# Two-layer hybrid decoder trunk: the first layer reads x channels first, scales by the norm's factors at the evictions, and runs its first chunk by rows of weights

## The chip, the cores and the metric

The kernel runs on one core of a Trainium2 chip. The metric is the device time of one execution in microseconds (us). Before the change three runs took 711.84, 712.14 and 716.08 us (median 712.14 us). TensorE is PE in the profile, VectorE is DVE, ScalarE is ACT, GpSimd is POOL, and SP is the engine whose queue issues the DMAs. TensorE's clock is granted at one of two levels, 1.2 or 2.4 GHz; the profile writes them as 0.5 and 1.0.

## The reference

The input x has 512 tokens of 1024 channels. Two layers follow each other, and each begins with an RMS norm and one wide projection:

```python
def rmsnorm(x, g, eps=RMS_EPS):
    xf = x.astype(jnp.float32)
    y = xf * lax.rsqrt(jnp.mean(xf * xf, axis=-1, keepdims=True) + eps)
    return (y * g.astype(jnp.float32)).astype(x.dtype)
...
    u = rmsnorm(h, norm_gain) @ w_in
    qa, ka, va, ga, qd, kd, vd, gd = jnp.split(u, list(np.cumsum(IN_SPLITS)[:-1]), axis=-1)
```

The eight parts have 512 columns each. Queries and keys get a partial rotation (rope) and feed two kinds of attention (a dilated window, "a", and a differential one, "d"); the values va and vd are multiplied by the attention weights; ga and gd gate the results through silu. An output projection, a second norm with a gate projection, and a small embedding product end the layer. A last norm ends the kernel. The norm multiplies each token by one factor (the inverse root mean square of its channels) and each channel by one gain, so that rmsnorm(h) @ w_in is the same as (h * gain) @ w_in with every token's row of the result multiplied by that token's factor.

## The kernel before

**Tiles.** The contraction over 1024 channels is cut into 8 blocks of 128 (kb). A weight *row* r is 256 input channels by 512 columns (kb 2r and 2r+1), 512 KB in one DMA; a *chunk* is four such rows. Each float32 number is split into a high part in TensorE's float32r form and a low part, the rest. A product takes three matmuls (high by high, high by low, low by high). A *unit* is one 128 x 512 result, 8 blocks of 3 matmuls, 24 in all. It is accumulated in one PSUM bank; units alternate between banks 0 and 1, and all else takes the other six banks in turn through `bank()`.

**Where a row goes.** SP loads it to a staging buffer (`stg`; the fourth load of all goes to `of`). ACT copies it to float32r (high part, 128 x 1024 at once), and then DVE or POOL subtracts (low part, in two halves of 128 x 512) into one of five slots of `ring`. A staging buffer is loaded again once both halves of its low part are done. `emit_loads` and `chunk` set this up. In the very first chunk DVE takes one half of each row and POOL the other; in later chunks POOL takes seven halves of eight.

**The order of chunks** is `SEQ`: vd (values), d0 and d1 (queries and keys of the differential heads), va, a0, a1, then the gates, the output projection (o0, o1) and the second norm's projection (p0, p1); 48 units in each layer, plus the attention of the heads in between.

**The order of instructions.** All operations are recorded first, with planned times (`pe` and `at`), and then `Machine.schedule` puts them in order with a list of costs of its own and replays them. So every instruction stands at line 286 of the profile (L286), and tiles name them. Within an engine instructions run in that fixed order; one that waits holds up those behind it.

**The start.** `warm_up` runs matmuls on zeros. SP loads x token by token (`load_x`, 128 tokens x 1024 channels each, tile `fr`), the norm's gain as one row, and the weights. `sumsq` and `rstd` make the token's factor: sums of squares on ACT and DVE, then a power of -0.5 on POOL (`st<-st 128x1`). `first_gain` spreads the gain over the partitions with POOL's partition_broadcast. `xn` multiplies x by factor and gain on DVE, TensorE transposes the result in 8 groups of 4 (`b<-idt,fr`), and ACT and DVE write its high and low parts to the tile `xy` (`norm_T`). Only then can the first chunk's matmuls run, a unit for each group of 128 tokens, and token group 1's norm is worked while unit 0 runs, and so on. The units of d0 come out with channels on the partitions; `qk_done` multiplies them by cos and sin tables, `v_done` splits the values, `gate_done` forms silu.

**Queues.** SP issues all DMAs in order. It holds at most eight open: each waits for the one eight places before it.

Of the kernel before, what the change touches and what calls it, by code (L numbers as in the profile page):

```python
# [312 lines left out]


def trunk(tc, x, p, attn_gain, w_in, w_out, lq1, lk1, lq2, lk2, subln, ple_gain, w_gate, w_ple,
          final_gain, tables, out):
    nc = tc.nc
    x2 = x.rearrange("b s d -> (b s) d")
    out2 = out.rearrange("b s d -> (b s) d")
# [4 lines left out]
    with tc.tile_pool(name="sb", bufs=1) as sb, tc.tile_pool(name="ps", bufs=1, space=PSUM) as psp, \  # L324
# [10 lines left out]
        OF = sb.tile([128, 8, 512], F32, name="of")  # L335
        MISC = sb.tile([128, 3, 512], F32, name="misc")
        CT = sb.tile([128, 4, 512], F32, name="ct")
        IDT = sb.tile([128, 128], F32, name="idt")
        ST = sb.tile([128, 192], F32, name="st")
        hsave = drp.tile([S, D], F32, name="hsave")  # L340
# [5 lines left out]
        GSUB = [ST[:, 8 + l:9 + l] for l in range(DEPTH)]  # L346
        SS = ST[:, 16:32]
        RS = ST[:, 32:36]
        VAR = ST[:, 36:40]
        DST = ST[:, 40:56]  # L350
        HST = ST[:, 64:128]
        GROW = MISC[0:1, 1:3, :].rearrange("p a n -> p (a n)")
        FRB = FR.rearrange("p (b n) -> p b n", n=512)

        def H(t, h):
# [53 lines left out]
        def emit_loads():  # L409
            order = sorted(range(len(loads)), key=lambda i: loads[i][:2])  # L410
            for n, i in enumerate(order):
                t, us, src, hi, lo, eng = loads[i]
                st = stage(n)

                def load(st=st, src=src):
                    SPQ.dma_start(st, src)

                def high(st=st, hi=hi):
                    ACT.activation(hi, st, AF.Copy)

                def low(k, st=st, hi=hi, lo=lo, eng=eng):
                    eng[k].tensor_sub(lo[:, k], st[:, k], hi[:, k])
                if n <= NSTG:
                    at(-10, 55.0 + 0.1 * n, load)
# [9 lines left out]
        def chunk(s0, src, k0=0):  # L434
            slots = {}
            for r in range(4):
                slot = npair[0] % NPAIR
                npair[0] += 1
                row = (r + k0 // 2) % 4
                slots[row] = slot  # L440
                if s0 == 0:
                    t, us = -10, 64.7 + 1.4 * r
# [38 lines left out]
        def rstd(t):  # L481
            DVE.tensor_scalar(VAR[:, t:t + 1], SS[:, 2 * t:2 * t + 1], SS[:, 2 * t + 1:2 * t + 2],
                              EPS, op0=OP.add, op1=OP.add)
            POOL.tensor_tensor(RS[:, t:t + 1], VAR[:, t:t + 1], NHALF[:, 0:1], op=OP.pow)

        def xn(t, h, gain):
            DVE.scalar_tensor_tensor(XN(t, h), H(t, h), RS[:, t:t + 1],
# [28 lines left out]
        def setup():  # L516
            DVE.memset(PT[:, 0, 0:512].bitcast(F32), 0.0)
            DVE.memset(NHALF, -0.5)
            for i in range(2):
                for e in range(2):  # L520
                    POOL.memset(QK[64 - 64 * e:128 - 64 * e, i, 4 + e].bitcast(F32), 0.0)
            ACT.activation(ST[:, 132:136], NHALF, AF.Exp)
            make_identity(nc, IDT)

        def load_x(t, h=None):
            cols = slice(0, D) if h is None else slice(512 * h, 512 * h + 512)
            SPQ.dma_start(HT(t)[:, cols], x2[t * 128:(t + 1) * 128, cols])

        def load_first_gain():
            SPQ.dma_start(GROW, attn_gain[0].unsqueeze(0))  # L530

        def first_gain():
            POOL.partition_broadcast(GN[0], GROW)


        def warm_up():
# [31 lines left out]
            at(-10, 60 + us, f, *a)  # L568

        st(-9, setup)  # L570
        st(-8, load_x, 0, 0)
        st(-7, load_x, 0, 1)
        st(-6, load_first_gain)
        for t in range(1, T):
            st((-4.75, -4, -3)[t - 1], load_x, t)
# [4 lines left out]
        st(2.0, first_gain)  # L580
        pe(-3, 6.0, warm_up)
        pe(-0.05, 1.2, lambda: None)
        for h in range(2):
            st(2.0 + 0.6 * h, sumsq, 0, h, (ACT, DVE)[h])
        norm_T(-10, 63.2, -0.9, 0, GN[0], 0)
        for t in range(1, T):
            for h in range(2):
                at(t - 1, 0.1 * h, sumsq, t, h, (ACT, DVE)[h])
            norm_T(t - 1, 1.0, t - 0.2, t, GN[0], 0)


        nP = [0]
# [174 lines left out]
        SHUF = list(range(8, 16)) + list(range(8)) + list(range(16, 32))  # L767
        nrt = [0]

        def qk_done(pr, isk):  # L770
            def done(t, o):
                r = {}
                buf = QK[:, pr % 2]

                def rot1():
                    r[0] = RT[nrt[0] % 2]
                    nrt[0] += 1
                    DVE.stream_shuffle(r[0][1], o, SHUF)
                    DVE.tensor_mul(r[0][0], o, C)

                def rot2():
                    POOL.tensor_mul(r[0][1], r[0][1], SN)
# [34 lines left out]
        def v_done(view, nh):  # L817
            def done(t, o):
                src = o.rearrange("p (h d) -> p h d", h=nh)

                def hi():
                    ACT.activation(view[:, :, 0, :], src, AF.Copy)

                def lo():
                    DVE.tensor_sub(view[:, :, 1, :], src, view[:, :, 0, :])
                at(t, 0.05, hi)
                at(t, 0.6, lo)
            return done

        def gate_done(kb, ureg, lo_from):  # L830
            def done(t, o):
                sg = MISC[:, 2, :]

                def f():
                    ACT.activation(sg, o, AF.Tanh, scale=0.5)
                    DVE.scalar_tensor_tensor(sg, sg, 1.0, o, op0=OP.add, op1=OP.mult)

                def g():
                    DVE.tensor_mul(OF[:, kb, :], OF[:, kb, :], sg)
# [75 lines left out]
        for l in range(DEPTH):  # L915
# [5 lines left out]
            def qk_chunk(name, g):  # L921
                s0 = at_of[name]
                w = chunk(s0, wi[CHUNK[name]])
                for n, c in enumerate((0, 2, 1, 3)):
                    unit(s0 + n, w, X, "col", c, qk_done(2 * g + n // 2, n % 2))

            def v_chunk(name, view, nh):
                s0 = at_of[name]
                w = chunk(s0, wi[CHUNK[name]])
                for t in range(T):  # L930
                    unit(s0 + t, w, X, "tok", t, v_done(view(Y, t), nh))

            def g_chunk(name, kb0):
                s0 = at_of[name]
                w = chunk(s0, wi[CHUNK[name]])
                for i in range(4):
                    unit(s0 + i, w, X, "col", i, gate_done(kb0 + i, Y, B + QA[7] + LP + 0.2))

            def o_chunk(name, h):
                s0 = at_of[name]  # L940
# [134 lines left out]
```

## Time and profile before

| | |
|---|---|
| median of three runs | 712.14 us (711.84 to 716.08) |
| the profiled execution | 715.25 us |
| its span, first to last instruction | 713.1 us |
| PE busy | 680.4 us, 95% of the span, 3379 matmuls and transposes |
| DVE, ACT, POOL busy | 428.0, 370.3, 359.7 us |
| mean granted clock of TensorE | 0.977 |

The span and 2.1 us around it make the profiled execution's own time. TensorE is busy in nearly all of the span. Busy time is an average over the whole program; the change's instructions stand in the first 80 us, apart from the evictions of layer 0.

### The profile page before, as it was taken

Reading aid. Unit: us, or ns where it says so; the run is one execution under the profiler, and the core shown is the slowest. Engines: PE = TensorE matmul, PEld = TensorE weight load, DVE = VectorE, ACT = ScalarE, POOL = GpSimd, SP = SyncE. Lnnn points to the kernel's source line nnn. Section 1 sums busy time; section 2 is a strip of 40 time slices with the busy share of each in tenths; the row PEclk is TensorE's granted clock in tenths of the full one; section 3 lists DMA queues with packets and bytes.
Section 4 is the critical chain, followed back from the end, with each engine's and each line's share of the span. In section 5 each row is a group of like instructions: output and inputs, shape, how many; then the busy total and the mean of one; then the engine's idle time right before and its main releaser. Section 6 shows DMA issues by size and latency. Waiting matters only on the chain.

```text
span 713.1 us, 9718 instructions
## 1 busy us (share of the span) xinstructions
PE 680.4 (95%) x3379; PEld 573.3 (80%) x3379; DVE 428.0 (60%) x855; ACT 370.3 (52%) x803; POOL 359.7 (50%) x279
## 2 busy tenths in 40 slices
PE   2399999999999999999999999999999999999995
PEld 1288888888888888888888888888888888888885
DVE  1573599675776573373364279976587657248244
ACT  2243556664887852443353255674578885244321
POOL 2327858086661343861552776717746154376122
PEclk7599999999999999999999999999999999999998
DMA  8214455134443354430432445414454344353002
GB/s 300 68 60 132 124 149 158 30 119 119 125 125 105 125 179 139 149 116 33 148 111 95 148 140 127 130 48 145 121 129 128 101 142 153 119 176 95 24 30 89
DMA packets 30883, 84.79 MB, mean 119 GB/s; under 512 B 5617, under 2 KB 5617, under 8 KB 30834
## 3 DMA queue, kind: packets, MB, share of 16 engines
q1 hardware_dynamic: 30834, 84.17, 38.5%
q8 instruction: 26, 0.43, 0.2%
q14 instruction: 23, 0.19, 0.1%
HBM read 63.18 MB, written 4.19 MB: 94 GB/s over the span
## 4 chain that ended last, share of the span: by engine, by line
PE 93%; issue 3%; DVE 2%; DMA 1%; POOL 0%; SPq 0%; POOLq 0%; ACT 0%; DVEq 0%
PE b L286 93%; DVE fr L286 2%; DMA stg<-in_w_in_dram 1%; SPq L286 0%; POOL of L286 0%; DVE pt L286 0%; DVE misc L286 0%; POOL st L286 0%; DVE of L286 0%; DVE ring L286 0%; POOLq L1071 0%; DVE st L286 0%; ACT of L286 0%; DVEq L1071 0%; POOLq L286 0%
## 5 line engine op out<-in xcount | busy, mean ns | idle before, releaser
L286 POOL TENSOR_TENSOR ring<-stg,ring 128x512 fp32r<-128x512 f32 x164 | 233.9, 1452 | 205.9 <-ACT ring L286 205.5
L286 PE MATMUL b<-xy,ring 128*128 128x512 f32 x1152 | 285.7, 394 | 0.0
L286 PE MATMUL b<-ring,xy 128*128 128x512 f32 (+1 forms) x1176 | 279.7, 391 | 0.0
L286 PEld LDWEIGHTS b<-ring,xy 128*128 128x128 f32 x1176 | 215.8, 189 | 41.6 <-DVE fr L286 0.2
L286 PEld LDWEIGHTS b<-xy,ring 128*128 128x128 f32 x1152 | 211.0, 188 | 39.1
L286 ACT ACTIVATE ring<-stg 128x1024 fp32r<-128x1024 f32 x95 | 100.0, 1058 | 55.0 <-PE b L286 39.4
L286 ACT ACTIVATE fr<-fr,st 128x128 f32<-128x128 f32 (+3 forms) x193 | 102.0, 556 | 34.3 <-DVE st L286 31.6
L286 DVE CUSTOM_DVE_ANT_0 fr<-b,ct 128x512 f32<-128x512 f32 (+3 forms) x128 | 58.4, 484 | 36.3 <-PE b L286 35.6
L286 PE MATMUL b<-idt,fr 128*128 128x128 f32 x368 | 53.2, 277 | 23.4 <-DVE fr L286 23.3
L286 POOL TENSOR_TENSOR fr<-fr,ct 128x512 f32<-128x512 f32 x32 | 44.4, 1386 | 57.0 <-DVE fr L286 57.0
L286 PEld LDWEIGHTS b<-idt,fr 128*128 128x128 f32 x368 | 45.2, 143 | 33.9 <-DVE fr L286 24.6
L286 DVE SCALAR_TENSOR_TENSOR fr<-fr,st,of 128x512 f32<-128x512 f32 (+1 forms) x39 | 44.0, 1161 | 25.8 <-POOL st L286 25.8
L286 ACT ACTIVATE xy<-b 128x512 fp32r<-128x512 f32 x48 | 28.3, 593 | 52.9 <-PE b L286 52.5
L286 DVE TENSOR_TENSOR ring<-stg,ring 128x512 fp32r<-128x512 f32 x26 | 32.6, 1253 | 36.5 <-ACT ring L286 36.5
L286 POOL TENSOR_TENSOR st<-st 128x1 f32<-128x1 f32 (+1 forms) x29 | 20.8, 718 | 63.3 <-DVE st L286 47.8
L286 PE MATMUL b<-qk 128*128 128x128 f32 (+3 forms) x256 | 52.7, 324 | 0.0
L286 DVE TENSOR_TENSOR pt<-b,pt 128x384 fp32r<-128x384 f32 (+1 forms) x72 | 40.0, 593 | 11.7 <-ACT pt L286 11.3
L286 POOL TENSOR_TENSOR fr<-fr 128x512 f32<-128x512 f32 x32 | 45.1, 1415 | 2.6 <-DVE fr L286 1.0
L286 ACT ACTIVATE fr<-fr 128x512 f32<-128x512 f32 x35 | 22.0, 629 | 46.6 <-DVE fr L286 44.3
L286 DVE TENSOR_TENSOR xy<-b,xy 128x512 fp32r<-128x512 f32 x48 | 32.4, 683 | 19.5 <-ACT xy L286 19.5
L286 ACT ACTIVATE pt<-b 128x384 fp32r<-128x384 f32 (+1 forms) x72 | 34.4, 524 | 18.2 <-PE b L286 18.1
L286 PEld LDWEIGHTS b<-qk 128*128 128x128 f32 x256 | 39.3, 190 | 4.0 <-issue 0.2
(62 smaller groups left out, 547.4 us busy)
## 6 DMA issues: line engine op xcount, KB each, us to landing
stg<-in_w_in_dram SPq DMA_DIRECT2D x63, 512.0 KB, 3.4
qk<-nt SPq DMA_DIRECT2D x128, 128.0 KB, 2.3
stg<-in_w_out_dram SPq DMA_DIRECT2D x16, 512.0 KB, 4.6
stg<-in_w_ple_gate_dram SPq DMA_DIRECT2D x16, 512.0 KB, 3.4
fr<-in_x_dram SPq DMA_DIRECT2D x7, 512.0 KB, 5.4
stg<-in_w_ple_dram SPq DMA_DIRECT2D x4, 512.0 KB, 3.3
hsave<-fr SPq DMA_DIRECT2D x4, 512.0 KB, 2.6
fr<-hsave SPq DMA_DIRECT2D x4, 512.0 KB, 3.4
```

The costliest lines, as they stand in the source:

```text
L286: getattr(self.eng[e], op)(*args, **kw)
```

## The change

The first layer no longer normalises x before its projection. The host hands x over a second time, transposed (`xt`, 128 x 8 x 512, channels on the partitions), and the gain with channels on the partitions (`gt`, 128 x 8, 32 bytes a partition). ACT writes the high part of x times gain straight into `xy`, DVE the low part. x by tokens is still loaded, for the sums of squares alone (`x_sumsq`). The factors of the tokens (`RS0`) are applied where the results leave PSUM: in `v_done` as a scale of each partition; for queries, keys and gates, where tokens lie along the free dimension, POOL puts the factors on the diagonals of four 128 x 128 matrices, four matmuls with a matrix of ones spread them over the partitions, and the cos and sin tables (`C0`, `SN0`) and a plain copy (`RB`) take them in (`spread_rstd`). Gates of layer 0 get one more DVE product. partition_broadcast, the eight groups of transposes and their evictions in layer 0 are gone. The first chunk runs by rows of weights: four PSUM banks are open, one for each token group, and each weight row is used for all four before the next. The warm-up has 14 matmuls in place of 11.

```diff
-        NWARM = 11
+        NWARM = 14
...
+        def units_by_rows(w, ureg, dones):
+            o = [BANK[0], BANK[1], bank(), bank()]
+            def part(r, t):
+                for kb in (2 * r, 2 * r + 1):
+                    for n, (ul, wl) in enumerate(PASSES):
+                        mm(o[t], UT(ureg, ul, kb)[:, t * 128:(t + 1) * 128], w(wl, kb),
+                           start=(kb == 0 and n == 0), stop=(kb == KB - 1 and n == 2))
+            for r in range(4):
+                for t in range(T):
+                    pe(r + 0.25 * t, 1.362, part, r, t)
+            for t in range(T):
+                dones[t](3.2 + 0.25 * t, o[t])
...
-        def first_gain():
-            POOL.partition_broadcast(GN[0], GROW)
+        def load_gt():
+            SPQ.dma_start(GT, gt)
+        def load_xt(r):
+            SPQ.dma_start(FRB[:, 2 * r:2 * r + 2, :], xt[:, 2 * r:2 * r + 2, :])
+        def xt_hi(kb):
+            ACT.activation(UT(0, 0, kb), FRB[:, kb, :], AF.Copy, scale=GT[:, kb:kb + 1])
+        def xt_lo(kb):
+            DVE.scalar_tensor_tensor(UT(0, 1, kb), FRB[:, kb, :], GT[:, kb:kb + 1], UT(0, 0, kb),
+                                     op0=OP.mult, op1=OP.subtract)
...
+        def spread_rstd():
+            b = bank()
+            for t in range(T):
+                diag = MISC[:, 1, t * 128:(t + 1) * 128]
+                POOL.tensor_scalar(diag, IDT, RS0[:, t:t + 1], None, op0=OP.mult)
+            for t in range(T):
+                mm(b[:, t * 128:(t + 1) * 128], ONES, MISC[:, 1, t * 128:(t + 1) * 128], start=True, stop=True)
+            ACT.activation(RB, b, AF.Copy)
+            DVE.tensor_mul(C0, C, b)
+            DVE.tensor_mul(SN0, SN, b)
...
-            norm_T(t - 1, 1.0, t - 0.2, t, GN[0], 0)
+                st(3.1 + 0.3 * t, x_sumsq, t, h)
+            st(3.2 + 0.3 * t, rstd, t, RS0)
+        pe(2.5, 1.9, spread_rstd)
...
-                    ACT.activation(view[:, :, 0, :], src, AF.Copy)
+                    ACT.activation(view[:, :, 0, :], src, AF.Copy, **({} if rs is None else {"scale": rs}))
...
+                    if l == 0:
+                        g = RT[1][kb % 2]
+                        DVE.tensor_mul(g, o, RB)
```

**PE, from the first instruction.** `pt` is the warm-up's zeros, `idt,fr` a transpose of x, `ring,xy` a matmul of the first chunk (vd), and the number after `b_` the PSUM bank. Before:

```order
L286 MATMUL b_79<-pt 128x512 x11
L286 MATMUL b_80<-idt,fr 128x128 x4
L286 MATMUL b_81<-idt,fr 128x128 x4
L286 MATMUL b_77<-ring,xy_63 128x512 x9
L286 MATMUL b_82<-idt,fr 128x128 x4
L286 MATMUL b_77<-ring,xy_63 128x512 x12
```

After, at the same place (the four groups of 6 are weight row 0 for the four token groups; rows 1 to 3 repeat them):

```order
L286 MATMUL b_84<-pt 128x512 x14
L286 MATMUL b_80<-ring,xy_63 128x512 x6
L286 MATMUL b_81<-ring,xy_63 128x512 x6
L286 MATMUL b_82<-ring,xy_63 128x512 x6
L286 MATMUL b_83<-ring,xy_63 128x512 x6
```

The transposes are gone, and the first real matmul needs one row of weights and two blocks of xt where it needed a normalised and transposed x.

**POOL, from the same place.** `qk` is a memset, the ISA row ahead of `of<-misc` and the one behind it reload POOL's code library around partition_broadcast, `st<-st` is the power that gives a token group's factors, `ring` a low half of weights. Before:

```order
L286 MEMSET qk 64x512 x3
L286 ISA
L286 ISA of<-misc 128x1024 [waits DMAHW2_49,Pool_49]
L286 ISA
L286 TENSOR_TENSOR st<-st 128x1 [waits DVE_49]
L286 TENSOR_TENSOR ring<-stg,ring 128x512 [waits DMAHW3_49,Activation_49]
```

After, the rows that follow the memset and the halves of the first chunk; the first four `ring` rows are the first two rows of d0, `misc<-idt,st` is a diagonal:

```order
L286 TENSOR_TENSOR ring<-stg,ring 128x512 [waits DMAHW2_49,Activation_49]
L286 TENSOR_TENSOR ring<-stg,ring 128x512
L286 TENSOR_TENSOR ring<-stg,ring 128x512 [waits DMAHW0_49,PE_49,Activation_49]
L286 TENSOR_TENSOR ring<-stg,ring 128x512 [waits PE_49]
L286 TENSOR_TENSOR st<-st 128x1 [waits DVE_49]
L286 TENSOR_SCALAR misc<-idt,st 128x128 [waits Pool_49]
L286 TENSOR_TENSOR st<-st 128x1 [waits DVE_49]
L286 TENSOR_SCALAR misc<-idt,st 128x128 [waits Pool_49]
L286 TENSOR_TENSOR ring<-stg,ring 128x512 [waits DMAHW3_49,PE_49,Activation_49]
L286 TENSOR_TENSOR ring<-stg,ring 128x512 [waits PE_49]
```

Both library reloads are gone, and the factors of token groups 2 and 3 stand between the second and the third weight row of d0.

**ACT, at the end of the first chunk after the change.** `xy_64<-b,st` is the eviction of a token group of vd with its factor, `ring<-stg` the high part of a weight row of d0, `fr,st<-fr` a sum of squares of token groups 2 and 3:

```order
L286 ACTIVATE xy_64<-b_81,st 128x4x128
L286 ACTIVATE ring<-stg 128x1024
L286 ACTIVATE fr,st<-fr 128x512 x2
L286 ACTIVATE xy_64<-b_82,st 128x4x128
L286 ACTIVATE xy_64<-b_83,st 128x4x128
L286 ACTIVATE ring<-stg 128x1024 x2
```

The evictions of groups 2 and 3, which wait for their factors, stand ahead of the third and fourth weight row of d0.

From the gates of layer 0 on, and in all of layer 1, PE's rows stand in the same order as before.

## Rows read from the trace of the kernel before

**Rows 1.** The page: span, and the clock in 40 equal slices (tenths of full speed).

```profile
span 713.1 us, 9718 instructions
...
PEclk7599999999999999999999999999999999999998
```

**Rows 2.** The waits of PE in the whole span: engine, line, waited for, us in total, times, longest.

```profile
PE b L286 <- DVE fr L286: 23.3, 2, 22.8
```

**Rows 3.** The timeline of the first 30 us: start, duration, engine, operation, out<-in, count, and idle time before it with what ended it.

```profile
1.47 4.30 PE L286 MATMUL b<-pt 128*128 128x512 f32 x11 [1.47 <-DVE pt L286]
1.57 2.20 POOL L286 MEMSET qk<- 64x512 f32 x4
...
14.48 1.30 POOL L286 PARTITION_BROADCAST of<-misc  x1 [10.71 <-issue]
...
26.12 0.59 POOL L286 TENSOR_TENSOR st<-st 128x1 f32<-128x1 f32 x1 [10.33 <-issue]
...
26.74 3.43 DVE L286 SCALAR_TENSOR_TENSOR fr<-fr,st,of 128x512 f32<-128x512 f32 x2 [17.69 <-POOL st L286]
...
28.55 1.11 PE L286 MATMUL b<-idt,fr 128*128 128x128 f32 x4 [22.78 <-DVE fr L286]
```

**Rows 4.** The timeline of PE from the first chunk to the second units of d0.

```profile
31.00 4.19 PE L286 MATMUL b<-ring,xy 128*128 128x512 f32 x9
34.98 0.84 PE L286 MATMUL b<-idt,fr 128*128 128x128 f32 x4
...
42.29 0.60 PE L286 MATMUL b<-idt,fr 128*128 128x128 f32 x4
...
42.64 2.33 PE L286 MATMUL b<-ring,xy 128*128 128x512 f32 x9
...
57.12 0.84 PE L286 MATMUL b<-xy,ring 128*128 128x512 f32 x3
...
58.48 16.71 PE L286 MATMUL b<-xy,ring 128*128 128x512 f32 x73
```

**Rows 5.** The same timeline further on, two rows.

```profile
74.80 5.60 PE L286 MATMUL b<-xy,ring 128*128 128x512 f32 x24
80.24 1.43 PE L286 MATMUL b<-qk 128*128 128x128 f32 x8
```

**Rows 6.** Stretches of the start: its length, busy time of PE, PEld, DVE, ACT, POOL (x instructions), granted clock, DMA share, GB/s.

```profile
7.00:8.00 1.00, 0.00 (x0) 0.00 (x0) 0.25 (x1) 0.72 (x1) 0.00 (x0) 1.00 1.06 426
8.00:9.00 1.00, 0.00 (x0) 0.00 (x0) 1.00 (x3) 0.72 (x2) 0.00 (x0) 0.58 0.97 385
...
34.00:35.00 1.00, 1.00 (x4) 0.61 (x4) 1.00 (x2) 0.00 (x0) 0.30 (x1) 0.50 0.00 0
35.00:36.00 1.00, 1.00 (x7) 0.96 (x6) 1.00 (x3) 0.14 (x1) 0.00 (x0) 0.77 0.30 37
36.00:37.00 1.00, 1.00 (x6) 0.82 (x5) 1.00 (x3) 1.00 (x3) 0.00 (x0) 1.00 0.80 287
```

**Rows 7.** The timeline of the first 20 us where it shows a landing: ACT's instructions that waited for a DMA, and SP's issues, each of which went out when the transfer eight places before it had landed.

```profile
4.10 0.63 ACT L286 ACTIVATE fr<-fr 128x512 f32<-128x512 f32 x1 [1.88 <-DMA fr<-in_x_dram]
...
6.66 1.06 ACT L286 ACTIVATE ring<-stg 128x1024 fp32r<-128x1024 f32 x1 [1.84 <-DMA stg<-in_w_in_dram]
...
8.16 0.63 ACT L286 ACTIVATE fr<-fr 128x512 f32<-128x512 f32 x1 [0.45 <-DMA fr<-in_x_dram]
...
9.44 1.06 ACT L286 ACTIVATE ring<-stg 128x1024 fp32r<-128x1024 f32 x1 [0.55 <-DMA stg<-in_w_in_dram]
...
10.72 0.33 SPq L286 DMA_DIRECT2D misc<-in_lambda_q_dram  x1
12.02 0.33 SPq L286 DMA_DIRECT2D misc<-in_lambda_k_dram  x1
13.28 0.33 SPq L286 DMA_DIRECT2D misc<-in_lambda_q_dram  x1
...
14.55 0.33 SPq L286 DMA_DIRECT2D misc<-in_lambda_k_dram  x1
15.98 0.33 SPq L286 DMA_DIRECT2D misc<-in_lambda_q_dram  x1
17.22 0.33 SPq L286 DMA_DIRECT2D misc<-in_lambda_k_dram  x1
17.59 1.83 SPq L286 DMA_DIRECT2D st<-in_subln_gain_dram  x2
```

**Rows 8.** Groups of instructions, shapes kept apart: busy us in all, mean ns of one, idle before them.

```profile
L286 POOL TENSOR_TENSOR ring<-stg,ring 128x512 fp32r<-128x512 f32 x164 | 233.9, 1452 | 205.9 <-ACT ring L286 205.5
L286 ACT ACTIVATE of<-b,st 128x512 f32<-128x512 f32 x8 | 5.5, 686 | 12.0 <-PE b L286 11.9
L286 DVE TENSOR_TENSOR fr<-b,ct 128x512 f32<-128x512 f32 x32 | 21.6, 676 | 0.2
masks.py:199 POOL TENSOR_SCALAR_AFFINE_SELECT idt<-idt 128x128 f32<-128x128 f32 x1 | 0.3, 292 | 0.3 <-POOL idt masks.py:197 0.3
```

**Rows 9.** The timeline: two DVE products with two operands in SBUF, the first beside a POOL product, the second not.

```profile
31.42 1.74 DVE L286 SCALAR_TENSOR_TENSOR fr<-fr,st,of 128x512 f32<-128x512 f32 x1
...
35.97 0.74 DVE L286 SCALAR_TENSOR_TENSOR fr<-fr,st,of 128x512 f32<-128x512 f32 x1
```

More of the change, by code (lines that the diff above doesn't have):

```diff
@@ L315, in trunk @@
 def trunk(tc, x, p, attn_gain, w_in, w_out, lq1, lk1, lq2, lk2, subln, ple_gain, w_gate, w_ple,
-          final_gain, tables, out):
+          final_gain, tables, xt, gt, out):
     nc = tc.nc
@@ L337, in trunk @@
         CT = sb.tile([128, 4, 512], F32, name="ct")
+        CR = sb.tile([128, 3, 512], F32, name="cr")
+        ONES = sb.tile([128, 128], F32, name="ones")
+        GT = sb.tile([128, KB], F32, name="gt")
         IDT = sb.tile([128, 128], F32, name="idt")
@@ L348, in trunk @@
         RS = ST[:, 32:36]
+        RS0 = ST[:, 136:140]
         VAR = ST[:, 36:40]
@@ L351, in trunk @@
         HST = ST[:, 64:128]
-        GROW = MISC[0:1, 1:3, :].rearrange("p a n -> p (a n)")
+        C0, SN0, RB = (CR[:, i, :] for i in range(3))
         FRB = FR.rearrange("p (b n) -> p b n", n=512)
@@ L423, in emit_loads @@
                 if n <= NSTG:
-                    at(-10, 55.0 + 0.1 * n, load)
+                    at(-10, 54.05 + 0.1 * n, load)
                 else:
@@ L479, in sumsq, with rstd @@
                                          op0=OP.mult, op1=OP.add, accum_out=acc)
-        def rstd(t):
+        def rstd(t, to=RS):
             DVE.tensor_scalar(VAR[:, t:t + 1], SS[:, 2 * t:2 * t + 1], SS[:, 2 * t + 1:2 * t + 2],
                               EPS, op0=OP.add, op1=OP.add)
-            POOL.tensor_tensor(RS[:, t:t + 1], VAR[:, t:t + 1], NHALF[:, 0:1], op=OP.pow)
+            POOL.tensor_tensor(to[:, t:t + 1], VAR[:, t:t + 1], NHALF[:, 0:1], op=OP.pow)
         def xn(t, h, gain):
@@ L522, in setup, with load_x, x_sumsq @@
             ACT.activation(ST[:, 132:136], NHALF, AF.Exp)
+            POOL.memset(ONES, 1.0)
             make_identity(nc, IDT)
[L525 to L530, printed above, removed]
-        def first_gain():
-            POOL.partition_broadcast(GN[0], GROW)
+        def load_gt():
[7 more added lines that the diff above has]
+                                     op0=OP.mult, op1=OP.subtract)
+        def load_x(t):
+            SPQ.dma_start(FR[:, 4096 + 1024 * (t % 2):5120 + 1024 * (t % 2)], x2[t * 128:(t + 1) * 128, :])
+        def x_sumsq(t, h):
+            v = FRB[:, 8 + 2 * (t % 2) + h, :]
+            acc = SS[:, 2 * t + h:2 * t + h + 1]
+            if h:
+                ACT.activation(v, v, AF.Square, scale=1.0 / 32, accum_out=acc)
+            else:
+                DVE.tensor_tensor_reduce(v, v, v, scale=1.0 / D, scalar=0.0, op0=OP.mult, op1=OP.add,
+                                         accum_out=acc)
+        def spread_rstd():
[8 more added lines that the diff above has]
+            DVE.tensor_mul(SN0, SN, b)
         def warm_up():
@@ L570, in trunk @@
         st(-9, setup)
[L571 to L575, printed above, removed]
+        st(-8.5, load_gt)
+        for r in range(4):
+            st(-6 + 0.1 * r, load_xt, r)
         at(0, 0.5, load_tables, 0)
@@ L579, in trunk @@
         at(3.5, 0, lambdas)
-        st(2.0, first_gain)
         pe(-3, 6.0, warm_up)
[L582 to L586, printed above, removed]
+        for kb in range(KB):
+            st(2.0 + 0.1 * kb, xt_hi, kb)
+            st(2.05 + 0.1 * kb, xt_lo, kb)
+        for t in range(T):
+            st(3.0 + 0.3 * t, load_x, t)
             for h in range(2):
-                at(t - 1, 0.1 * h, sumsq, t, h, (ACT, DVE)[h])
-            norm_T(t - 1, 1.0, t - 0.2, t, GN[0], 0)
+                st(3.1 + 0.3 * t, x_sumsq, t, h)
+            st(3.2 + 0.3 * t, rstd, t, RS0)
+        pe(2.5, 1.9, spread_rstd)
         nP = [0]
@@ L768, in trunk, with qk_done @@
         nrt = [0]
-        def qk_done(pr, isk):
+        def qk_done(pr, isk, l):
+            cos, sin = (C, SN) if l else (C0, SN0)
             def done(t, o):
@@ L778, in rot1 @@
                     DVE.stream_shuffle(r[0][1], o, SHUF)
-                    DVE.tensor_mul(r[0][0], o, C)
+                    DVE.tensor_mul(r[0][0], o, cos)
                 def rot2():
-                    POOL.tensor_mul(r[0][1], r[0][1], SN)
+                    POOL.tensor_mul(r[0][1], r[0][1], sin)
                     POOL.tensor_add(r[0][0], r[0][0], r[0][1])
@@ L815, in qk_done, with v_done @@
             return done
-        def v_done(view, nh):
+        def v_done(view, nh, rs):
             def done(t, o):
@@ L821, in hi @@
                 def hi():
-                    ACT.activation(view[:, :, 0, :], src, AF.Copy)
+                    ACT.activation(view[:, :, 0, :], src, AF.Copy, **({} if rs is None else {"scale": rs}))
                 def lo():
-                    DVE.tensor_sub(view[:, :, 1, :], src, view[:, :, 0, :])
+                    if rs is None:
+                        DVE.tensor_sub(view[:, :, 1, :], src, view[:, :, 0, :])
+                    else:
+                        DVE.scalar_tensor_tensor(view[:, :, 1, :], src, rs, view[:, :, 0, :],
+                                                 op0=OP.mult, op1=OP.subtract)
                 at(t, 0.05, hi)
@@ L828, in v_done, with gate_done @@
             return done
-        def gate_done(kb, ureg, lo_from):
+        def gate_done(kb, ureg, lo_from, l):
             def done(t, o):
@@ L834, in f @@
                 def f():
-                    ACT.activation(sg, o, AF.Tanh, scale=0.5)
-                    DVE.scalar_tensor_tensor(sg, sg, 1.0, o, op0=OP.add, op1=OP.mult)
+                    g = o
+                    if l == 0:
+                        g = RT[1][kb % 2]
+                        DVE.tensor_mul(g, o, RB)
+                    ACT.activation(sg, g, AF.Tanh, scale=0.5)
+                    DVE.scalar_tensor_tensor(sg, sg, 1.0, g, op0=OP.add, op1=OP.mult)
                 def g():
@@ L929, in v_chunk @@
                 w = chunk(s0, wi[CHUNK[name]])
+                dones = [v_done(view(Y, t), nh, None if l else RS0[:, t:t + 1]) for t in range(T)]
+                if s0 == 0:
+                    units_by_rows(w, X, dones)
+                    return
                 for t in range(T):
-                    unit(s0 + t, w, X, "tok", t, v_done(view(Y, t), nh))
+                    unit(s0 + t, w, X, "tok", t, dones[t])
             def g_chunk(name, kb0):
@@ L1064 @@
     arrays, args = {}, []
-    for name in _INS + ["tables"]:
-        a = const_tables() if name == "tables" else layout(name, inputs[name])
+    for name in _INS + ["tables", "xt", "gt"]:
+        if name == "xt":
+            a = np.ascontiguousarray(np.asarray(inputs["x"])[0].T.reshape(KB, 128, S).transpose(1, 0, 2))
+        elif name == "gt":
+            a = np.ascontiguousarray(np.asarray(inputs["attn_norm_gain"])[0].reshape(KB, 128).T)
+        else:
+            a = const_tables() if name == "tables" else layout(name, inputs[name])
         arrays[f"in_{name}_dram"] = a
```

6 lines of the change are left out of this document (3 added, 3 removed).

## The prediction

> **What bounds the kernel now.** I read the page first: the span is 713.1 us, and the clock row has its low figures in the first slices and the last [rows 1]. Then PE's waits: of 23.3 us in all, one wait of 22.8 us on DVE is nearly the whole [rows 2]. So PE is a stream without holes that starts late. The timeline of the start says why [rows 3]. The warm-up ends at 5.77 us, and PE's next instruction starts at 28.55. It waited for DVE, whose product waited 17.69 us for POOL's one-column power. POOL itself waited for nothing that the profile shows: 10.71 us of "issue" ahead of partition_broadcast, which runs only 1.30 us, and 10.33 us of "issue" behind it, ahead of the power. In the program a reload of POOL's library stands at each of these two places. So of the 28.55 us, 21 are two code loads.
>
> The clock adds to it. It fell to 1.2 GHz between 8 and 9 us, in the idle stretch, and came back only between 35 and 36 us, 7 us after PE had restarted [rows 6]. At the low level nine matmuls took 34.98 - 31.00 = 3.98 us, 0.442 each [rows 4]; at the high level 24 took 80.24 - 74.80 = 5.44 us, 0.227 each [rows 5]. From 31.00 to 58.48 PE did the 96 matmuls of the first chunk and three of d0, with transposes between them [rows 4], so the first chunk's end is worth 58.48 - 0.68 = 57.8 us. The first two units of d0, 48 matmuls at 0.227, would end at 68.7.
>
> **The change: when PE can start.** Transfers land one 512 KB after the other: the first at 4.10, the second at 6.66, then 8.16, 9.44, 10.72, 12.02, 13.28, 14.55, 15.98 and 17.22 [rows 7]. The change issues as many at the same pace in another order: w0, xt0, gt, w1, xt1, x0, x1, w2, xt2, w3, xt3, the tables. I give each the landing of its place: w0 4.1, xt0 6.7, w1 8.2, xt1 9.4, w2 13.3, xt2 14.6, w3 16.0, xt3 17.2. gt is 128 pieces of 32 bytes; the nearest rows are the two small subln loads, 1.83 us of issue for both, which SP has to spare here. I let it land with xt0; the next place, 8.2, is its upper bound. ACT has split w0 by then (1.06 us). The high parts of xt0 are scaled copies, 0.69 us each as for the scaled eviction [rows 8]: 7.4 and 8.1. The low parts are DVE products of two SBUF operands, 0.74 us, or 1.74 beside POOL [rows 9]; near the start POOL has half of w0 alone, so I take 0.74: 8.1 and 8.9. PE starts at 7.4, and the first six matmuls end at 9.1, two of them behind the last low part.
>
> The other 90 run at 0.227 if the rows keep coming: 24 matmuls, 5.4 us, to a row. A row is ready at most 3.5 us after its xt (two copies and two products at 0.69 and about 1): row 1 at 12.9, row 2 at 18.1, row 3 at 20.7. They are wanted at 13.2, 18.6 and 24.1. So the chunk ends at E = 9.1 + 20.4 = 29.5 us, and 57.8 - 29.5 = **28.3 us** are gained. In it are the eight groups of transposes, 0.35 us each by 42.64 - 42.29 [rows 4], 2.8 us in all; the slow clock, 7 us at about half rate, some 3.3; the remainder is the wait. The three further warm-up matmuls lie in the wait for xt0.
>
> **What is late next: d0.** In the old order its weights had 28 us of idle engines ahead of them. In the new one ACT and POOL reach them when the first chunk is already ending. SP issues d0's first row when xt3 has landed (17.2), and its second behind the lambda and subln loads, about 22.4; they land near 21 and 26, in time. ACT takes in order: eviction 0 (possible at E - 4.1), high part of row 0, eviction 1, row 1, the two squares of token groups 2 and 3 (0.63 us each [rows 7]), then eviction 2, which waits for POOL's factor. With 0.69 and 1.06 us row 0 is split at E - 2.35 and row 1 at E - 0.6. POOL, at 1.45 us a half [rows 8], ends row 0's low part at E + 0.55, row 1's at E + 3.45, and only then makes two powers (0.59 us [rows 3]) and two diagonals (between 0.3, the select of this shape, and 0.75; I take 0.4): E + 5.4. ACT's eviction 3 follows, then row 2's high part at E + 6.8, and POOL's halves at E + 8.25 and 9.7, row 3's at E + 11.2. PE needs 2.7 us for a row of two units. It runs rows 0 and 1 without a wait until E + 5.4, then the four matmuls with ones (between one transpose group, 0.35, and four times that; I take 1.0), waits for row 2's low part until E + 8.25 but for one matmul, and ends the two units at E + 13.6. Dense it would be 10.9: **2.7 us** are lost, 1.0 for the ones and 1.7 waiting. The bounds are no wait at all and, if ACT and POOL are each later by what they are queued behind, some 6.
>
> The rest costs nothing that I can see. Four evictions with a scale take 0.69 us for 0.60 and lie beside PE. The gates of layer 0 add eight DVE products of 0.68 us [rows 8]; each frees its bank earlier than the tanh did, and PE waits 0.5 us outside the start [rows 2]. Were the cover gone, it is 5.4 us. The 2 MB of xt take SP's and the DMAs' time ahead of the tables, which d0 needs only at E + 7. From the gates on PE's order is that of before.
>
> **Sum.** 28.3 - 2.7 = 25.6 us. The profiled execution took 715.25, so 689.7. That execution is 3.1 us above the median shown. If those 3.1 lie in the start (code loads, the clock's return), they go with it and 689.7 stands; if not, the median would be 686.6.
>
> **A rule to weigh.** The idle rows give 10.7 and 10.3 us to the code loads [rows 3]. The Trainium skill, GPSIMD Engine Reference, 2.1 Instruction dispatch, says that the first call to a newly loaded kernel pays an instruction-memory load of about 6 us that no instruction in the profile shows. The trace agrees that it shows none, and has 4 to 5 us more at each place. By the rule 12 us would be code and 9 something else that may stay in front of the first power; since the values' evictions and not PE's start hang on the power now, I keep the rows' reading and carry the other as a rival.
>
> **Rivals.**
> 1. *The clock falls again* between the warm-up's end, about 6.5 us, and the dense part at 9. It fell in the old start some 2.5 us after PE had stopped, and came back 7 us after the restart [rows 6]. Here the gap is about 1 us, with six matmuls in the next 1.7. If it falls, 7 us at half rate cost 3.4: 693.
> 2. *POOL and ACT bound d0 more than I reckon*, by products of 1.74 where DVE and POOL run together, evictions later than their factors, or a second dip of the clock: 4 to 8 us more, 694 to 698.
> 3. *9 us of POOL's idle time are not code* and stay ahead of the first power, which stands ahead of half of w2 and w3 on POOL. Factor 0 would come at 13 + 9 = 22, w2's half at about 25 for 18.6: 6 to 9 us, 696 to 699.
> 4. *No faster, or slower: the clock stays at 1.2 GHz while the matmuls come row by row.* Each matmul costs 0.215 us more, so the gain is gone after 25.6/0.215 = 119 matmuls, the first chunk and half of the two d0 units; with all 144 it is 5 us slower, 721. Against it: at 0.442 us a row lasts 10.6 us and the next is there in half that, so PE would not wait, and after 28.55 the clock did come back with PE no denser [rows 6]. The Trainium skill, TensorE: Matmul & The Clock Gate, Loop structure matters more than you think, speaks against loops that wait for a DMA between matmuls, since PE goes cold in them; this loop is nearer to that than the old one, and by it this rival would be the likely one.
>
> **Chances and numbers.** My forecast, 689.7 (its own range 686.5 to 693), 0.66; rival 1, 0.14; rival 2, 0.12; rival 3, 0.04; rival 4, 0.04. The range runs to the ends of the first two rivals, and down to the median's reading of the sum: 686 to 697. A measurement of this kernel tells about 1%, 7 us, from no change; all but rival 4 are beyond that on the fast side: faster 0.96, same 0.02, slower 0.02.
>
> **What would show it.** Right: no idle "issue" of 10 us on POOL, PE's first chunk from about 7.4 to about 29.5 us in groups of six without a wait between rows, a PE wait of 1 to 3 us near 35 to 38 on POOL's `ring` behind the power, PE's two d0 units done near 43, and the same stream from there. Wrong: a clock of 0.5 beyond 10 us, PE waiting on `xy` or `ring` between rows, an idle POOL ahead of its first power, or new PE waits at the gates of layer 0.

## The result, and the profile after

The change made the kernel faster: 694.15 us (median of four runs, 693.96 to 694.79) against 712.72 us before (four runs on the same chip, 711.84 to 716.08), a ratio of 0.9733 with a 95% interval of 0.970 to 0.9766. The medians are 18.6 us apart. The profiled executions, from which the sum was made, are 715.25 - 694.23 = 21.0 us apart, since the one of before lay 2.5 us above its median and the one of after lies on it.

The page of the changed kernel: span, busy time of the engines, and the clock in 40 slices, which answers to [rows 1].

```profile
span 692.3 us, 9689 instructions
...
PE 679.1 (98%) x3358; PEld 568.9 (82%) x3358; DVE 439.1 (63%) x857; ACT 370.9 (54%) x804; POOL 362.4 (52%) x283
...
PEclk9999999999999999999999999999999999999999
```

The low digits at the start are gone, and PE is idle for 13 us in all (692.3 - 679.1), where it was 33. Its waits (engine, line, waited for, us in total, times, longest) answer to [rows 2]:

```profile
PE b L286 <- DVE fr L286: 2.0, 3, 1.4
...
PE b L286 <- POOL ring L286: 0.9, 1, 0.9
PE b L286 <- ACT ring L286: 0.5, 1, 0.5
```

The wait of 22.8 us is gone, and small ones have come. The timeline of the first 20 us, against [rows 3] (start, duration, engine, operation, out<-in, count, idle time before it and what ended it):

```profile
1.44 5.71 PE L286 MATMUL b<-pt 128*128 128x512 f32 x14 [1.44 <-DVE st L286]
...
6.59 1.34 ACT L286 ACTIVATE xy<-fr,gt 128x512 fp32r<-128x512 f32 x2 [1.38 <-DMA gt<-in_gt_dram]
...
7.36 22.42 PE L286 MATMUL b<-ring,xy 128*128 128x512 f32 x96 [0.21 <-ACT xy L286]
...
8.40 1.57 SPq L286 DMA_DIRECT2D ct<-in_tables_dram  x2
...
13.57 0.93 POOL L286 TENSOR_TENSOR st<-st 128x1 f32<-128x1 f32 x1 [2.22 <-DVE st L286]
```

PE runs all 96 matmuls of the first chunk as one block, 0.2 us behind the warm-up's modelled end, from 7.36 us on. POOL's first power starts 12.5 us earlier than in [rows 3], and its idle time has a releaser, DVE, not "issue". From 29.6 to 55 us, rows of PE, ACT and DVE, and one of POOL:

```profile
29.62 5.60 PE L286 MATMUL b<-xy,ring 128*128 128x512 f32 x24
...
34.06 0.69 ACT L286 ACTIVATE xy<-b,st 128x512 fp32r<-128x512 f32 x1 [2.21 <-POOL st L286]
...
35.06 0.83 PE L286 MATMUL b<-misc,ones 128*128 128x128 f32 x6
...
36.04 0.49 PE L286 MATMUL b<-misc,ones 128*128 128x128 f32 x2
...
36.99 0.49 PE L286 MATMUL b<-xy,ring 128*128 128x512 f32 x1 [0.47 <-ACT ring L286]
...
38.36 5.86 PE L286 MATMUL b<-xy,ring 128*128 128x512 f32 x23 [0.87 <-POOL ring L286]
...
38.78 1.31 DVE L286 CUSTOM_DVE_ANT_0 misc<-misc 128x64 f32<-128x64 f32 x1
...
40.13 1.21 DVE L286 CUSTOM_DVE_ANT_0 misc<-misc 128x64 f32<-128x64 f32 x1
...
41.22 1.29 POOL L286 TENSOR_TENSOR ring<-stg,ring 128x512 fp32r<-128x512 f32 x1
...
41.38 1.20 DVE L286 CUSTOM_DVE_ANT_0 misc<-misc 128x64 f32<-128x64 f32 x1
...
42.63 1.20 DVE L286 CUSTOM_DVE_ANT_0 misc<-misc 128x64 f32<-128x64 f32 x1
...
44.26 0.72 DVE L286 STREAM_SHUFFLE fr<-b 128x512 f32<-128x512 f32 x1
...
45.61 9.81 PE L286 MATMUL b<-xy,ring 128*128 128x512 f32 x42 [1.39 <-DVE fr L286]
```

The first two units of d0 are the 24 + 1 + 23 matmuls from 29.62 to 44.22. ACT's eviction of token group 2 at 34.06 waited for POOL's power; behind it on ACT stand the high parts of d0's next rows, and PE waits for them (0.47) and for the low part (0.87). Then PE waits again, 1.39 us, for the rotation of the first pair (`fr<-b`), which DVE can start only at 44.26: ahead of it stand four sums for the lambdas (scalars of the attention), 1.2 to 1.3 us each for 64 columns. Before the change the last of these sums started at 49.22 us, beside the first chunk and well ahead of d0's first unit:

```profile
49.22 0.22 DVE L286 CUSTOM_DVE_ANT_0 misc<-misc 128x64 f32<-128x64 f32 x1
```

How much of the gain is left at each place can be read where both kernels have done the same matmuls:

| Place on PE | before | after | gain |
|---|---|---|---|
| first chunk done (after); the same number of matmuls (before) | 57.8 | 29.6 | 28.2 |
| first two units of d0 done | 68.7 | 44.2 | 24.5 |
| next matmul of d0 starts | 68.7 | 45.6 | 23.1 |
| third group of `b<-idt,misc` | 151.3 | 129.6 | 21.7 |
| profiled execution's own time | 715.25 | 694.23 | 21.0 |

The two times of 68.7 are worked out in the prediction. The fourth row is this one, first of before, then of after:

```profile
151.26 0.66 PE L286 MATMUL b<-idt,misc 128*128 128x128 f32 x4
```

```profile
129.59 0.66 PE L286 MATMUL b<-idt,misc 128*128 128x128 f32 x4
```

### The profile page after: what moved, and what is told of

Same layout as the page of the kernel before. It is cut to its first block, busy times and chain, and to the rows that moved or that the text cites. A ratio compares the mean times of both kernels' runs of the same rounds, so it can differ in the third digit from the quotient of the medians.

```text
span 692.3 us, 9689 instructions
## 1 busy us (share of the span) xinstructions
PE 679.1 (98%) x3358; PEld 568.9 (82%) x3358; DVE 439.1 (63%) x857; ACT 370.9 (54%) x804; POOL 362.4 (52%) x283
## 4 chain that ended last, share of the span: by engine, by line
PE 69%; issue 10%; POOL 9%; DMA 6%; DVE 5%; ACT 1%; SPq 0%; POOLq 0%; DVEq 0%; ACTq 0%
PE b L286 69%; POOL ring L286 6%; DVE fr L286 3%; DMA stg<-in_w_in_dram 1%; DMA stg<-in_w_out_dram 1%; POOL fr L286 1%; DMA stg<-in_w_ple_dram 1%; DMA fr<-in_xt_dram 1%; DMA qk<-nt 1%; POOL st L286 1%; SPq L286 0%; POOL misc L286 0%; DVE xy L286 0%; DVE misc L286 0%; DVE st L286 0%
## 5 line engine op out<-in xcount | busy, mean ns | idle before, releaser
L286 PE MATMUL b<-ring,xy 128*128 128x512 f32 (+1 forms) x1176 | 276.9, 388 | 0.5 <-ACT xy L286 0.2
L286 ACT ACTIVATE fr<-fr,st 128x512 f32<-128x512 f32 (+3 forms) x193 | 101.9, 556 | 38.8 <-DVE st L286 35.9
L286 PEld LDWEIGHTS b<-idt,fr 128*128 128x128 f32 x336 | 40.3, 140 | 10.3 <-DVE fr L286 2.4
L286 PE MATMUL b<-idt,fr 128*128 128x128 f32 x336 | 47.3, 273 | 0.7 <-DVE fr L286 0.6
L286 DVE TENSOR_TENSOR pt<-b,pt 128x384 fp32r<-128x384 f32 (+1 forms) x72 | 40.1, 592 | 11.2 <-ACT pt L286 10.7
L286 DVE SCALAR_TENSOR_TENSOR fr<-fr,st,of 128x512 f32<-128x512 f32 (+1 forms) x31 | 35.2, 1170 | 9.2 <-POOL st L286 9.2
L286 POOL TENSOR_TENSOR fr<-fr,ct 128x512 f32<-128x512 f32 x16 | 22.2, 1387 | 31.8 <-DVE fr L286 31.8
L286 POOL TENSOR_TENSOR fr<-fr,cr 128x512 f32<-128x512 f32 x16 | 21.4, 1342 | 30.5 <-DVE fr L286 30.5
L286 ACT ACTIVATE nt<-fr 128x512 fp32r<-128x512 f32 x32 | 19.7, 624 | 31.3 <-POOL fr L286 31.3
```

Of the source, the lines that this page charges most:

```text
L286: getattr(self.eng[e], op)(*args, **kw)
```

## The experiments

Two theories stood against each other. A, that of the prediction: the gain is the two code loads of POOL and the slow clock behind them; the order by rows starts PE early, and d0, whose weights are split late, gives some back. B: the idle time on POOL was only partly code, or the clock would not hold row by row, so that the gain has another source.

In experiments 1 to 4 the kernel before took 712.76 us (seven runs, 711.92 to 714.28), as beside the changed kernel (712.72), so differences to its 694.15 are taken directly.

**1. Only the code loads gone.** The kernel before, with its gain spread by a DMA to all partitions in place of partition_broadcast; norm, transposes and order stay.

```diff
-            SPQ.dma_start(GROW, attn_gain[0].unsqueeze(0))
+            load_gain(0, attn_gain[0])
...
-        st(2.0, first_gain)
```

> The kernel before, with one thing changed: the first gain is spread over the partitions by a DMA (as later gains are) and not by partition_broadcast, so no code library is reloaded. x is still normalised and transposed. Theory A (the two code loads made nearly all of PE's 22.8 us wait): the first factor is there near 6 us, PE's transposes start at 7.5 to 9 us, weight rows land one place later (w0 8.2, w1 10.7, w2 12.0, w3 13.3), unit 0 ends near 17, and the first chunk near 35 us for 57.8 before; d0 is as dense as before. 715.25 - 22.6 = 693 us, up to 696 with the clock low at the start. So the reload alone would be worth as much as the whole change. Theory B (some 9 of the 21 us of idle POOL are not code, as a load of 6 us would have it): the first factor comes near 15 us, and the time is 701 to 705.

Measured: 699.07 us (698.5 to 699.17) against 712.76 before, ratio 0.9803 (0.9787 to 0.9819): 13.7 us faster, between the two expectations. Its timeline:

```profile
5.56 0.56 POOL L286 TENSOR_TENSOR st<-st 128x1 f32<-128x1 f32 x1 [1.99 <-DVE st L286]
...
8.64 1.41 DVE L286 SCALAR_TENSOR_TENSOR fr<-fr,st,of 128x512 f32<-128x512 f32 x2 [3.23 <-DMA of<-in_attn_norm_gain_dram]
...
9.45 1.97 PE L286 MATMUL b<-idt,fr 128*128 128x128 f32 x8 [2.91 <-DVE fr L286]
...
16.50 0.66 PE L286 MATMUL b<-idt,fr 128*128 128x128 f32 x4 [2.15 <-DVE fr L286]
...
42.27 0.84 PE L286 MATMUL b<-ring,xy 128*128 128x512 f32 x3
...
42.95 7.42 PE L286 MATMUL b<-xy,ring 128*128 128x512 f32 x32
```

The first power starts at 5.56 us where it was 26.12 [rows 3]: the 20 us ahead of it were the reloads. PE starts at 9.45, behind the gain's landing, has holes of 2 us, and is at d0 with the same number of matmuls 42.95 - 30.3 = 12.7 us later than the changed kernel (29.62 and three matmuls). Its d0, however, runs dense, since its weights were ready, and the two kernels end only 4.9 us apart. So the reloads alone are worth about three quarters of the whole gain, and the other parts of the change, which bring PE to d0 12.7 us earlier still, keep less than half of that. One more line, the stretch from 18 to 20 us (columns as in [rows 6]):

```profile
18.00:20.00 2.00, 1.82 (x4) 1.49 (x5) 2.00 (x5) 0.73 (x1) 1.19 (x1) 0.50 0.44 128
```

The clock stood at 1.2 GHz here, after PE had been idle for 2.15 and 0.79 us; it was at 2.4 GHz again from about 21.2. So this kernel loses some time at the low level too, which is neither the reloads nor a wait.

**2. By units instead of by rows.** The changed kernel without

```diff
-                if s0 == 0:
-                    units_by_rows(w, X, dones)
-                    return
```

> The changed kernel, but its first chunk runs a unit for each token group (24 matmuls in one bank) and not by rows of weights. Theory A (rows let PE work while weights arrive): unit 0 cannot end before the fourth row is split, near 21 us, and three units of 5.4 us follow, so the first chunk ends near 38 to 39 us for 29.6; weights of d0 are then in time and the 2 to 4 us of waits there go. 699 to 702 us. Rival (the order of the first chunk does not matter, since all that counts is that PE starts early): 693 to 695.

Measured: 700.36 us (699.88 to 701.59), ratio 0.9825 (0.9807 to 0.9844), 6.2 us slower than the changed kernel, in the range of A. PE, with one row of ACT, and then a stretch of 1 us:

```profile
10.46 0.73 PE L286 MATMUL b<-ring,xy 128*128 128x512 f32 x2 [4.15 <-ACT xy L286]
...
24.71 11.18 PE L286 MATMUL b<-ring,xy 128*128 128x512 f32 x48 [0.95 <-DVE xy L286]
...
38.33 0.69 ACT L286 ACTIVATE xy<-b,st 128x512 fp32r<-128x512 f32 x1 [2.84 <-POOL st L286]
...
39.86 1.65 PE L286 MATMUL b<-xy,ring 128*128 128x512 f32 x3 [3.97 <-DVE xy L286]
```

```profile
43.00:44.00 1.00, 1.00 (x4) 0.81 (x4) 0.69 (x1) 0.03 (x1) 1.00 (x2) 0.50 0.00 0
```

PE starts 3.1 us later, and the chunk is done at 24.71 + 11.18 = 35.9 us, 6.1 us behind the changed kernel (7.36 + 22.42 = 29.8). Then PE waits 4.0 us, where A had d0's waits gone: d0's first unit takes bank 0, which here holds token group 2 until its factor is there (ACT's row), and behind that wait the clock stood at 1.2 GHz until about 45 us. d0's first matmul comes 10.2 us later; 6.2 of them stay. So A's time came true and its steps only in part, and the run takes away the order by rows together with the four open banks; what each is worth alone is not shown.

**3. No warm-up.** `NWARM = 14` becomes 0.

> The changed kernel without the 14 warm-up matmuls. Theory A (the first chunk is dense enough to bring the clock up by itself, as after the restart at 28.55 us before, where it took 7 us): PE starts at 7.4, the clock is at 1.2 GHz for 3 to 7 us of it, 696 to 698 us. Rival (matmuls that come row by row leave the clock low, so the warm-up is what keeps the first chunk fast): 1.2 GHz through the chunk, 96 matmuls at 0.442 us, 712 us or more.

Measured: 695.43 us (695.3 to 696.93), ratio 0.9758 (0.974 to 0.9777), 1.3 us slower than the changed kernel and just under A's 696 to 698. First PE's row, then two stretches of 1 us:

```profile
7.51 24.19 PE L286 MATMUL b<-ring,xy 128*128 128x512 f32 x96 [7.51 <-ACT xy L286]
```

```profile
9.00:10.00 1.00, 1.00 (x4) 0.81 (x3) 0.28 (x1) 0.77 (x2) 0.24 (x1) 1.00 1.05 430
...
12.00:13.00 1.00, 1.00 (x6) 0.83 (x5) 1.00 (x3) 0.54 (x1) 0.00 (x0) 1.00 1.03 422
```

The number behind x counts the matmuls whose records touch the stretch: four at 1.2 GHz and six at 2.4 GHz in [rows 6], and four here until 12 us, six from there. In the trace PE's matmuls start 0.427 us apart until 12 us and 0.227 apart from 12.5. The clock column says 1.00 for both; the matmuls show the lower level, the column does not. The rival in which the clock stays low row by row is refuted: 4.5 us after a cold start it was high, while the rows of weights still came from the DMAs one after the other.

**4. The broadcast kept beside the change.** The changed kernel also loads the gain row and runs POOL's partition_broadcast early; nothing reads the result.

```diff
+        st(-8.4, load_first_gain)
+        st(-5.0, first_gain)
```

> The changed kernel with the old partition_broadcast left in, of a gain row that nothing reads. It stands on POOL behind the half of w2, ahead of the diagonals and the half of w3, at about 16 us. Theory A (each of the two code loads is about 10 us): POOL is away until about 38 us, PE stops in row 3 of the first chunk near 25 us and goes on near 40, d0 waits less; 15 to 18 us more than the changed kernel, 709 to 712. Theory B (6 us a load): away until about 30, PE goes on near 32, 700 to 703 us.

Measured: 706.99 us (706.79 to 709.49), ratio 0.9926 (0.9899 to 0.9953), 12.8 us slower than the changed kernel, between the two expectations. POOL's rows, and PE's:

```profile
25.21 1.30 POOL L286 PARTITION_BROADCAST of<-misc  x1 [9.20 <-issue]
34.78 1.20 POOL L286 TENSOR_SCALAR misc<-idt,st 128x128 f32<-128x128 f32 x2 [8.27 <-issue]
...
37.27 7.47 PE L286 MATMUL b<-ring,xy 128*128 128x512 f32 x20 [11.91 <-POOL ring L286]
```

Put into a kernel in which everything else runs early, the two reloads make idle "issue" of 9.2 and 8.3 us again, and PE waits 11.9 us for a weight half behind them. So the time does belong to the reloads. They are nearer to the 10.7 and 10.3 of [rows 3] than to the 6 us of the Trainium skill (GPSIMD Engine Reference, 2.1 Instruction dispatch), and there are two of them, there and back.

Not all of the 12.8 us is waiting: behind the wait 13 of PE's 20 matmuls came at the pace of 1.2 GHz.

**5. The changed kernel again**, beside the next three, on another chip (before: 714.24 us there).

> The changed kernel once more, on the chip of the next three, so that a microsecond or two between them can be read: 694 us, within 0.5.

Measured: 694.11 us (692.41 to 694.92), ratio 0.9713 (0.9694 to 0.9732). Its profiled execution (693.63 us) is a second trace of the same kernel. A stretch of 1 us, and the load of the weights for the third unit of d0 (PEld):

```profile
39.00:40.00 1.00, 1.00 (x3) 0.76 (x3) 0.97 (x3) 0.34 (x1) 1.00 (x2) 0.50 0.00 0
```

```profile
45.30 1.68 PEld L286 LDWEIGHTS b<-xy,ring 128*128 128x128 f32 x8 [0.53 <-DVE fr L286]
```

In this execution the clock fell behind the two waits in d0 and stood at 1.2 GHz from about 38.5 to 41.9 us. The last matmul of the first pair started at 44.81 us, where it was 43.83, and hardly any of the 1.39 us wait is left. The next unit still started at 45.30, for 45.61: in both traces it had to wait for the rotation, which DVE started behind the four sums (43.95 and 44.26). So the fall of the clock cost nothing here.

**6. Buffers of their own for x of token groups 2 and 3.** In the change the x of groups 2 and 3 goes into the buffers of groups 0 and 1 and is loaded behind them. Here it goes to a free part of `of`:

```diff
+        def XV(t):
+            return FRB[:, 8 + 2 * t:10 + 2 * t, :] if t < 2 else OF[:, 2 * (t - 2):2 * (t - 2) + 2, :]
...
-            SPQ.dma_start(FR[:, 4096 + 1024 * (t % 2):5120 + 1024 * (t % 2)], x2[t * 128:(t + 1) * 128, :])
+            SPQ.dma_start(XV(t), x2[t * 128:(t + 1) * 128, :].rearrange("p (a n) -> p a n", a=2))
...
-            v = FRB[:, 8 + 2 * (t % 2) + h, :]
+            v = XV(t)[:, h, :]
```

> The changed kernel with buffers of their own for the tokens' x of groups 2 and 3, so that their loads go out ahead of w3 and xt3 and all four factors are made before d0's weights reach POOL. In the order the four lambda sums come to stand ahead of the evictions on DVE too. Theory A (in d0 PE waits because factors 2 and 3 stand between d0's second and third weight row on POOL, and evictions 2 and 3 ahead of its third on ACT): the waits at 36 to 38.4 us go, 1.7 us, and with the lambda sums the 1.4 us at 44 too: 691 us. Rival (POOL's 2.9 us a weight row against PE's 2.7 is the bound there): 693.5 to 694.

Measured: **690.28 us** (690.09 to 690.28), ratio 0.9662 (0.9647 to 0.9676), 3.8 us faster than the changed kernel beside it, and faster than both kernels. Timeline, PE and DVE:

```profile
24.16 1.05 PE L286 MATMUL b<-misc,ones 128*128 128x128 f32 x8
...
27.08 0.22 DVE L286 CUSTOM_DVE_ANT_0 misc<-misc 128x64 f32<-128x64 f32 x1
...
28.60 1.19 DVE L286 CUSTOM_DVE_ANT_0 misc<-misc 128x64 f32<-128x64 f32 x1
...
30.50 3.11 PE L286 MATMUL b<-xy,ring 128*128 128x512 f32 x13
33.82 16.37 PE L286 MATMUL b<-xy,ring 128*128 128x512 f32 x69 [0.21 <-POOL ring L286]
...
42.19 1.91 PEld L286 LDWEIGHTS b<-xy,ring 128*128 128x128 f32 x9 [0.47 <-DVE fr L286]
```

All factors are ready before the chunk ends, so the matmuls with ones lie inside it, ACT's evictions wait for no factor, and the first pair of d0 has one wait, of 0.21 us. The third unit starts at 42.19 us, 45.61 - 42.19 = 3.4 us earlier than after the change and 3.1 us earlier than in the trace of experiment 5; the medians differ by 3.8. The run moves the factors and the sums together, so it does not tell their shares apart. The lambda sums come here while POOL is idle and take 0.22 us; the one that runs beside a POOL product takes 1.19.

**7. Lambda sums earlier.** To see whether the 1.39 us wait is theirs:

```diff
-        at(3.5, 0, lambdas)
+        st(12.0, lambdas)
```

> The changed kernel with the four lambda sums recorded while the first chunk runs, so that on DVE they stand among its products and no longer between the last half of d0's weights and the rotation of d0's first unit. Theory A (PE's wait of 1.4 us at 44 is for that rotation, queued behind four sums of 64 columns that took 1.2 us each beside POOL, for 0.2 alone): the wait goes, 692.7 us. Rival (the rotation is late for another reason, such as the units that end together): 694.

Measured: 694.09 us (693.3 to 695.51), ratio 0.9718 (0.9701 to 0.9735): no difference to the changed kernel. The rotation no longer stands behind the sums: it starts when the first unit of d0 is ready, and PE has no wait of 1.39 us for it. That the sums held it up is so shown. But their DMAs went ahead with them on SP, past the loads of the two tables, which now go out at 20.31 us (8.40 after the change) and land just ahead of d0's second row:

```profile
20.31 0.81 SPq L286 DMA_DIRECT2D ct<-in_tables_dram  x2
...
30.61 1.06 ACT L286 ACTIVATE ring<-stg 128x1024 fp32r<-128x1024 f32 x1 [2.93 <-DMA stg<-in_w_in_dram]
...
37.72 0.49 PE L286 MATMUL b<-misc,ones 128*128 128x128 f32 x2 [0.76 <-POOL misc L286]
...
40.03 10.29 PE L286 MATMUL b<-xy,ring 128*128 128x512 f32 x41 [0.86 <-POOL ring L286]
```

ACT waits 2.93 us for d0's second row, and the diagonals are late too (0.76). The gain was given back a few microseconds ahead of where it was made: the third unit of d0 starts at 45.93 us.

**8. Both.**

> Both of the last two. Theory A: the same as the own buffers alone, 691 us, as these move the lambda sums already; if the buffers alone leave one of the two waits, 1.4 us less than they. Rival: 693.5 to 694.

Measured: 696.09 us (695.78 to 697.72), ratio 0.9742 (0.9726 to 0.9758), slower than either; the expectation failed.

```profile
28.36 0.23 DVE L286 CUSTOM_DVE_ANT_0 misc<-misc 128x64 f32<-128x64 f32 x1 [1.59 <-DMA misc<-in_lambda_k_dram]
28.52 0.75 DVE L286 SCALAR_TENSOR_TENSOR xy<-fr,gt,xy 128x512 fp32r<-128x512 f32 x1
...
29.79 2.07 PE L286 MATMUL b<-misc,ones 128*128 128x128 f32 x8 [5.42 <-POOL misc L286]
```

DVE waits for each lambda's DMA with the last low parts of xt queued behind it, and PE stands 5.42 us ahead of the matmuls with ones, whose diagonals share the tile `misc` with the lambdas (the last diagonal is written behind the last sum).

## Why the prediction was nearly right, point by point

- **What bounds the kernel: right.** The 21 us of "issue" on POOL were the two reloads: without them the power comes at 5.6 us (experiment 1), and with them put back the idle time is there again (experiment 4). Rival 3 is refuted: in the changed kernel no such idle time is left.
- **When PE starts, and the first chunk: right.** 7.36 and 29.62 us, for 7.4 and 29.5; gain 28.2 for 28.3. No wait stands between the rows, and the order by rows, with its four open banks, is worth 6.2 us (experiment 2).
- **The clock: right.** In the profiled execution the matmuls came at the pace of 2.4 GHz from the warm-up's last three on (rival 1 did not come). Even cold the clock rose after eleven matmuls (rival 4 refuted, experiment 3). The second dip that rival 2 names did come in the trace of experiment 5, behind the waits in d0, and cost nothing. The Trainium skill's warning of loops that wait for a DMA (TensorE: Matmul & The Clock Gate, Loop structure matters more than you think) speaks of a long DMA wait between the matmuls; it did not apply, since PE did not wait between the rows.
- **What d0 loses: mis-sized.** This is the term that failed. The prediction has d0's first pair at E + 13.6, "1.0 for the ones and 1.7 waiting", 2.7 us lost. Against dense units the pair lost 44.22 - 29.62 - 10.9 = 3.7: the ones with the holes beside them took 1.5, the two waits 1.3, and 0.9 lie in longer matmuls next to the waits (0.49 for the one at 36.99, 5.86 for the 23 behind it). The mechanism, factors 2 and 3 on POOL and the evictions behind them on ACT, was the one told, and experiment 6 shows it: with the factors early the two waits shrink to one of 0.21 us.
- **Behind the pair: a wait that the prediction did not have.** It let the stream of before go on at 43.1. PE waited 1.4 us more for DVE's rotation behind the lambda sums (experiments 5 and 7 show that they held the rotation up). In the old order the sums were done by 49.4 us, beside the first chunk; the prediction moved their DMAs and forgot the sums. Another 1.4 us went between 45 and 130 us, of which three waits of PE for DVE show 0.8; the rest, and the last 0.7 up to the end, stay unexplained. (From the third group of `b<-idt,misc` to the end the two traces of the changed kernel take 692.3 - 129.6 = 562.7 and 691.7 - 128.4 = 563.3 us, so 0.6 us there is a difference between two executions.) Together 1.1 + 1.4 + 1.4 + 0.7 = 4.6 us, the difference of 25.6 and 21.0.
- **Gates: right.** PE shows no wait for their products.
- **Rival 2** (POOL and ACT bound d0 more, 694 to 698) came true in time, at the lower end of its range, and in half its mechanism. The measured 694.2 lies outside the forecast's own 686.5 to 693; the stated range of 686 to 697 holds it because it takes this rival in. The evictions were later than reckoned, and DVE beside POOL was slow, but on the lambda sums, not on the products named.
- **The median.** The prediction asked whether the excess of before's profiled execution lay in the start. The forecast of 689.7 is 4.5 us below the time after, by the profile and by the median. The gain of 25.6 us is 4.6 above the 21.0 of the profiled executions and 7.0 above the 18.6 of the medians: the other 2.4 us are the excess of before's profiled execution, which the sum took in. Where in before that excess lay, no run tells.

## What to carry to other kernels

Idle "issue" ahead of and behind a POOL instruction that needs another library is a price of that instruction, paid twice; here a DMA that does its job brought three quarters of the gain alone. When a start is pulled forward, list everything that the old order did on each engine ahead of the next stage, the sums and evictions as well as the loads: it all comes back a little later. A small buffer that is shared between early and late loads can decide when a factor is ready; two more of them were worth 3.8 us here, and moving the waiting work itself was worth nothing because its DMAs moved with it, ahead of loads that were needed sooner.

## What the runs showed of the hardware that was not expected

- DVE's sum over 64 columns with two SBUF operands takes 0.22 us while POOL is idle and 1.2 to 1.3 us beside a POOL product, five to six times as long, where the 512-column product of [rows 9] took 0.74 and 1.74. The extra is the rest of the POOL product that was running: the sum at 41.38 ended at 42.58, and POOL's product from 41.22 at 42.51. All four sums after the change end 0.07 to 0.08 us behind a POOL product, and so does the slow one of experiment 6. So here a short sum beside a stream of POOL products of 1.3 us costs about one of them.
- A reload of POOL's library took 10.7 and 10.3 us in the old start and 9.2 and 8.3 us in experiment 4. That neighbours on the DMA queues make the difference was not tried.
- The clock column of a stretch read 1.00 while matmuls came at the spacing of 1.2 GHz (experiment 3, before 12 us, and the first ten of the warm-up after the change): look at the distance of the matmuls as well.
